# Inner norms of a two-layer decoder trunk: order of the first scaled and modulated pieces, a constant product on another engine, and eight instead of four weight units held back at the end

## The chip, the core and the metric

The kernel runs on one core of a Trainium2 chip. A core has five engines that run their own instruction lists in order and wait for each other by semaphores: TensorE (PE, matrix products and transposes; its weight loads are listed apart as PEld), VectorE (DVE), ScalarE (ACT), GpSimd (POOL) and SyncE (SP, which issues most transfers). Weights lie in HBM and come to the on-chip memory (SBUF) by DMA; TensorE writes its sums to eight banks of PSUM. The metric is the time of one execution in microseconds (us). The kernel before takes 2213.51 us (median of 3 runs, 2211.17 to 2214.28).

## What is computed

x has 256 rows (tokens) of 2048. Each of two layers has a token mixer (forgetting attention in layer 0, sliding-window attention in layer 1) and a gated feed-forward network with a causal convolution. Every such part is framed in the same way; the shift, scale and gate come from a conditioning vector c:

```python
c_act = jax.nn.silu(c)
for i in range(DEPTH):
    mod = c_act @ ada_w[i] + ada_b[i]
    sh1, sc1, g1, sh2, sc2, g2 = jnp.split(mod[:, None, :], 6, axis=-1)
    h = x * (1.0 + sc1) + sh1
    ...  # y = attention(h)
    x = layer_norm(DEEPNORM_ALPHA * x + (1.0 + g1) * y, ln_mix_g[i], ln_mix_b[i])
    h = x * (1.0 + sc2) + sh2
    y = conv_ffn(h, ffn_w_up[i], ffn_conv_w[i], ffn_conv_b[i], ffn_w_down[i])
    x = layer_norm(DEEPNORM_ALPHA * x + (1.0 + g2) * y, ln_ffn_g[i], ln_ffn_b[i])
return x
```

So there are four layer norms. After three of them, the inner ones, the normalised x is scaled, shifted and multiplied with the next weights; the last one gives the output.

## The kernel before

**Numbers in two parts.** All large products are made in a reduced float32 format. To keep the precision, each operand is split into a high part (the value cast to that format) and a low part (value minus high part), and a product is three matmuls: high by high, low by high, high by low. For a weight tile `w`, ScalarE makes the high part `wh` (a cast, line 268), VectorE the low part `wl` (a subtraction, line 279). In the activations the two halves are called hH and hL; both lie in one tile, `hpad`, and the profile names both "hH".

**Units.** Weights stream in units of 256 contraction rows by 512 columns (512 KB each). A unit is 24 matmuls of 256 columns where weights are stationary (`w_mm`, outputs named `ws`) or 12 matmuls of 512 columns where activations are (`x_mm`, outputs `xs`; six of them for each half t of the 256 tokens). Four buffers hold `wh` and four `wl`, so the cast of a unit waits until TensorE is done with the unit four places before. Ten buffers hold the raw weights.

**Order of the work.** The program is written by functions that queue work; a scheduler then fixes the order on each engine by its own estimates, except that instructions wrapped in `pin(...)` keep their program order among the pinned ones of their engine.

**An inner norm** runs at the three places where one part ends and the next begins. The last block's sum for token half t = 0 and then for t = 1 goes through `residual`: VectorE multiplies by the gate (line 632), adds to x (634), takes statistics (639, 642, 644), and GpSimd raises the variance to the power -1/2 (645). For t = 0 the product -mean times that factor (638) is made on VectorE, pinned between the two halves' work. `between` then calls `modulate`: x is normalised in four column blocks d of 512 (t = 0 on ScalarE, line 655; t = 1 on VectorE, line 657), TensorE transposes it in pieces of 128 by 128 (496; tile `sm`; a piece of 128 columns over both token halves is called a chunk here, there are 16), and `mod_pair` scales and shifts a chunk. For chunks 0 to 3 ScalarE writes hH straight from the transpose (506) and VectorE computes the value again (507) and subtracts (508) to get hL. For the later chunks, two at a time, ScalarE (510) and VectorE (511) make one chunk each, ScalarE casts both (84) and VectorE subtracts (85). These later pairs ("feeds") are queued one behind each unit of the next product. `spin` issues small matmuls without use on TensorE: three while it waits for the statistics, two behind the first transposes.

**The end.** In the last product of a part the last units are held back (`x_mm_end`): their matmuls for t = 0 run first, then those for t = 1, so that the residual of t = 0 runs beside the matmuls of t = 1. In the last product of the kernel four units are held. After the last residual the output is x minus mean, times gain (line 1180), times the factor, plus bias (1181), in four blocks for each t, each stored by a DMA.

Of the kernel before, what the change touches and what calls it, by code (L numbers as in the profile page):

```python
# [11 lines left out]
F32R = mybir.dt.float32r  # L12
I32 = mybir.dt.int32
AF = mybir.ActivationFunctionType
ALU = mybir.AluOpType
AX = mybir.AxisListType

P = 128
D = 2048
S = 256  # L20
# [21 lines left out]
def hybrid_trunk(ctx: ExitStack, tc: tile.TileContext, a: dict, out: bass.AP):  # L42
# [34 lines left out]
    def pin(ins, on=True):  # L77

        if on:
            tc.keep_in_program_order(ins)  # L80
# [176 lines left out]
        while post:  # L257
            run_post()

    def stream(wsrc, row0, col, ks, use):  # L260

        for kc in ks[::2]:
            r0 = (row0 + kc) * P
            w = wtile()
            pin(nc.sync.dma_start(w, wsrc[r0:r0 + 2 * P, col:col + WB].rearrange("(k p) f -> p k f", p=P)), False)
            h = hl.tile([P, 2, WB], F32R, tag="wh", name="wh")
            l = hl.tile([P, 2, WB], F32R, tag="wl", name="wl")
            pin(nc.scalar.copy(h, w), False)  # L268

            def go(kc=kc, h=h, l=l):  # L270
                ahead[0] -= 1
                run_post()
                use(kc, h, l)
                if feeds:
                    feeds.pop(0)()
                tick()

            def residual_(w=w, h=h, l=l, go=go):
                pin(nc.vector.tensor_tensor(l, w, f32(h), op=ALU.subtract), behind[0] > 0)  # L279
                behind[0] -= 1  # L280
                del residuals[go]

            ahead[0] += 1
            weights.add(go)
            residuals[go] = residual_
            work.append(go)
            settle(2)
# [25 lines left out]
    def w_mm(ps, kc, h, l, last=KC - 1, first=0):  # L313

        for i in range(2):
            for f in range(4):
# [3 lines left out]
                mm(o, wh, hL[:, kc + i, :], skip_group_check=True)  # L320
                mm(o, wl, hH[:, kc + i, :], stop=kc + i == last, skip_group_check=True)

    def x_stationary(wsrc, col, k0, nk, stat, end=0):

        ps = x_banks()
        use = x_mm_end(ps, stat, nk, end) if end else lambda kc, h, l: x_mm(ps, kc, h, l, stat, nk - 1)
        stream(wsrc, k0, col, list(range(nk)), use)
        return ps

    def w_stationary(wsrc, col):  # L330
# [166 lines left out]
            os.append(o)  # L497
        return os

    def mod_pair(G, B, k, ps, fast=False, keep=False):  # L500
        tmp = ttile()
        if fast:
            for j in range(2):
                o = tmp[:, j * S:(j + 1) * S]
                g, b = G[:, k + j:k + j + 1], B[:, k + j:k + j + 1]
                pin(nc.scalar.activation(hH[:, k + j, :], ps[j], AF.Identity, bias=b, scale=g), keep)
                nc.vector.tensor_scalar(o, ps[j], g, b, op0=ALU.mult, op1=ALU.add)
                nc.vector.tensor_tensor(hL[:, k + j, :], o, f32(hH[:, k + j, :]), op=ALU.subtract)
            return
        pin(nc.scalar.activation(tmp[:, :S], ps[0], AF.Identity, bias=B[:, k:k + 1], scale=G[:, k:k + 1]), keep)  # L510
        nc.vector.tensor_scalar(tmp[:, S:], ps[1], G[:, k + 1:k + 2], B[:, k + 1:k + 2],
                                op0=ALU.mult, op1=ALU.add)
        split(hH[:, k:k + 2, :], hL[:, k:k + 2, :], tmp.rearrange("p (j s) -> p j s", j=2))
# [4 lines left out]
    def spin(o, n):  # L518

        for _ in range(n):  # L520
            pin(mm(o[:, :3 * P], ident, mask.rearrange("p a b -> p (a b)"), start=True, stop=True))

    def modulate(G, B, norm, o=None):

        def feed(k):
            if k % 4 == 0:
                norm(k // 4)
            mod_pair(G, B, k, mod_turn(k, 2), k < 4)

        feeds.extend([lambda k=k: feed(k) for k in range(0, KC, 2)])  # L530
        for _ in range(2):
            feeds.pop(0)()
        spin(o, 2)

    def opening(plan, proj, prep):

# [92 lines left out]
    def residual(ps, d, gate, last):  # L629
        for t in range(NT):  # L630
            tmp = ttile()
            nc.vector.tensor_tensor(tmp, ps[t], gate[:, d * 512:(d + 1) * 512], op=ALU.mult)  # L632
            xs = x[:, t, d * 512:(d + 1) * 512]
            nc.vector.tensor_tensor(xs, xs, tmp, op=ALU.add)  # L634
            if last:
                if t == 1 and d == D // 512 - 1:
                    mu, rs, nm = moments[0]
                    pin(nc.vector.scalar_tensor_tensor(nm, mu, -1.0, rs, op0=ALU.mult, op1=ALU.mult))  # L638
                nc.vector.bn_stats(stats[:, t, d, :], xs)  # L639
                if d == D // 512 - 1:  # L640
                    mv = sp.tile([P, 2], F32, tag="mv", name="mv")
                    nc.vector.bn_aggr(mv, stats[:, t].rearrange("p a b -> p (a b)"))  # L642
                    rs = sp.tile([P, 2], F32, tag="rs", name="rs")
                    nc.vector.tensor_scalar_add(mv[:, 1:2], mv[:, 1:2], EPS)  # L644
                    nc.gpsimd.tensor_tensor(rs[:, 0:1], mv[:, 1:2], mhalf, op=ALU.pow)
                    moments[t] = (mv[:, 0:1], rs[:, 0:1], rs[:, 1:2])
            yield

    def normalise(d):

        for t in range(NT):
            mu, rs, nm = moments[t]
            xs = x[:, t, d * 512:(d + 1) * 512]
            if t == 0:
                nc.scalar.activation(xs, xs, AF.Identity, scale=rs, bias=nm)
            else:
                nc.vector.tensor_scalar(xs, xs, mu, rs, op0=ALU.subtract, op1=ALU.mult)

    def ln_rows(name, l):
        gb, bb = [], []  # L660
# [425 lines left out]
    def conv_ffn(l):  # L1086
        w_up, w_dn = a["ffn_w_up"][l], a["ffn_w_down"][l]
        NB = DFF // WB
        cw = lambda j, f: ccol[:, l, j, f:f + 1]

        def conv(pf, f):
            u = tp.tile([P, S], F32, tag="u", bufs=3, name="u")
            nc.scalar.activation(u, pf, AF.Identity, bias=cw(CW, f), scale=cw(2, f))  # L1093
            nc.vector.scalar_tensor_tensor(u[:, 1:], pf[:, :S - 1], cw(1, f), u[:, 1:],  # L1094
                                           op0=ALU.mult, op1=ALU.add)
            nc.vector.scalar_tensor_tensor(u[:, 2:], pf[:, :S - 2], cw(0, f), u[:, 2:],  # L1096
                                           op0=ALU.mult, op1=ALU.add)
            return u

        def evac(ps, f0, then):  # L1100
            u = None
            for f in range(5):
                v = conv(ps[f // 2][:, f % 2, :], f0 + f) if f < 4 else None
                if u is not None:
                    then(f - 1, u)
                u = v
                yield
                yield

        def silu(sil):  # L1110
            def f_(f, u):
                nc.scalar.activation(sil[f // 2][:, (f % 2) * S:(f % 2 + 1) * S], u, AF.Silu)
            return f_

        def gated(sil, gT):
            def f_(f, u):
                nc.vector.tensor_tensor(u, u, sil[f // 2][:, (f % 2) * S:(f % 2 + 1) * S], op=ALU.mult)
                g = gtile("gT")
                split(g[:, 0, :], g[:, 1, :], u)
                gT.append(g)  # L1120
            return f_

        sbs = [(0, 6), (6, NB)]
        for si, (b0, b1) in enumerate(sbs):
            gT = []
            then(lambda: ada.update(rate=(0.64, 0.4)[l]))
            for b in range(b0, b1):
                ps = w_stationary(w_up, b * WB)
                sil = [ttile("sil") for _ in range(2)]
                then(lambda ps=ps, b=b, sil=sil: defer(evac(ps, b * 4, silu(sil))))  # L1130
                ps = w_stationary(w_up, DFF + b * WB)
                then(lambda ps=ps, b=b, sil=sil, gT=gT: defer(evac(ps, DFF // P + b * 4, gated(sil, gT))))

            def stat(kc, t, gT=gT):
                while kc >= len(gT):
                    run_post()
                return gT[kc][:, 0, t * P:(t + 1) * P], gT[kc][:, 1, t * P:(t + 1) * P]

            def ready(si=si):
                if si == 0:  # L1140
                    drain()
                ada_need(l, 5)
                ada["rate"] = (0.95, 0.4)[l]

            then(ready)
            for d in range(D // WB):
                ps = x_stationary(w_dn, d * WB, b0 * 4, (b1 - b0) * 4, stat, (2, 4)[l] if si > 0 and d == D // WB - 1 else 0)
                then(lambda ps=ps, d=d, si=si: defer(residual(ps, d, gates[l, 5], si == len(sbs) - 1)),
                     si > 0 and d == D // WB - 1)
        then(lambda: (flush(), ada.update(gate_free=True)), True)  # L1150
# [58 lines left out]
```

## Time and profile before

| | |
|---|---|
| median of the runs shown | 2213.51 us |
| the profiled execution | 2215.89 us |
| its span, first to last instruction | 2214.0 us |
| TensorE busy | 2164.3 us (98%) |
| VectorE busy | 1792.8 us (81%) |
| ScalarE busy | 1159.6 us (52%) |
| GpSimd busy | 19.0 us (1%) |
| mean granted TensorE clock | 0.992 |

The three inner norms lie near 471, 1208 and 1470 us, the end near 2190 to 2214 us. A row of the timeline has the start, the length, the engine, the line, the operation, the tiles (written <- read), their shape and how many instructions are merged in it; in brackets stands how long the engine had been idle and what released it. The length of a merged row runs from the first start to the last end. Line numbers are those of the kernel before.

### The profile page before, as it was taken

How to read it: one execution, taken by the hardware profiler on the slowest of the kernel's cores; microseconds unless marked ns; L12 is line 12 of the kernel's file. 1: busy time of each engine (PE TensorE's matmuls, PEld its weight loads, DVE VectorE, ACT ScalarE, POOL GpSimd, SP SyncE). 2: the span in 40 equal slices, each digit the busy share in tenths (PEclk: the TensorE clock that was granted, in tenths of full speed). 3: DMA queues.
4: the chain of work that ended last, by engine and by line, in shares of the span. 5: the costliest groups of instructions: out<-in, count | busy, mean ns of one | idle time of the engine just before them, and what ended most of it. 6: DMA issues, size and time to landing. Idle time of an engine off the chain costs nothing. (4 is left out here: it accounts for less than half of the span.)

```text
span 2214.0 us, 38357 instructions
## 1 busy us (share of the span) xinstructions
PE 2164.3 (98%) x14915; PEld 1976.7 (89%) x14915; DVE 1792.8 (81%) x2459; ACT 1159.6 (52%) x1841; POOL 19.0 (1%) x48
## 2 busy tenths in 40 slices
PE   6999999999999999999999999999999999999997
PEld 5999888789999988999987877789999988999986
DVE  6879998989978979799798888789888655666756
ACT  3435656465565543655644677555555533555532
POOL 0000000000000000000000000000000000000000
PEclk9999999999999999999999999999999999999999
DMA  9999998979978989899797676678888566666663
GB/s 334 368 352 366 351 352 298 327 257 323 349 234 300 322 312 385 260 311 322 251 354 290 201 240 206 208 257 295 281 264 270 187 194 195 192 195 195 191 195 108
DMA packets 274246, 602.98 MB, mean 272 GB/s; under 512 B 21062, under 2 KB 29960, under 8 KB 273552
## 3 DMA queue, kind: packets, MB, share of 16 engines
q1 hardware_dynamic: 273008, 595.85, 79.6%
q0 software_dynamic: 1056, 4.69, 0.6%
q8 instruction: 116, 1.90, 0.3%
q14 instruction: 66, 0.54, 0.1%
HBM read 598.37 MB, written 2.10 MB: 271 GB/s over the span
## 5 line engine op out<-in xcount | busy, mean ns | idle before, releaser
L268 ACT CAST wh<-w 128x1024 fp32r<-128x1024 f32 x728 | 765.3, 1053 | 790.0 <-PE ws L75 284.5
L75 PE MATMUL ws<-hH,wh 128*128 128x256 f32 x6656 | 1153.3, 278 | 4.6 <-ACT hH L84 2.1
L279 DVE TENSOR_TENSOR wl<-w,wh 128x1024 fp32r<-128x1024 f32 x728 | 887.6, 1222 | 325.3 <-ACT wh L268 308.5
L75 PEld LDWEIGHTS ws<-hH,wh 128*128 128x128 f32 x6656 | 1012.1, 189 | 9.0 <-ACT hH L84 2.3
L75 PE MATMUL ws<-hH,wl 128*128 128x256 f32 x3328 | 918.6, 277 | 4.3 <-DVE wl L279 4.0
L75 PEld LDWEIGHTS ws<-hH,wl 128*128 128x128 f32 x3328 | 628.5, 189 | 6.0 <-DVE wl L279 5.9
L75 PE MATMUL xs<-wh,gT 128*128 128x512 f32 x1408 | 435.3, 389 | 0.0
L75 PEld LDWEIGHTS xs<-wh,gT 128*128 128x128 f32 x1408 | 264.3, 188 | 54.7
L75 PE MATMUL xs<-wl,gT 128*128 128x512 f32 x704 | 273.9, 389 | 0.0
L75 PE MATMUL xs<-wh,hH 128*128 128x512 f32 x704 | 235.9, 401 | 0.0
L397 DVE SCALAR_TENSOR_TENSOR acc<-wa,cact,acc 128x1024 f32<-128x1024 f32 x180 | 228.4, 1278 | 0.0
L397 DVE SCALAR_TENSOR_TENSOR acc<-wa,cactp,acc 128x1024 f32<-128x1024 f32 x128 | 162.3, 1278 | 0.3 <-DMA acc<-in_ada_b_dram 0.3
L75 PEld LDWEIGHTS xs<-wh,hH 128*128 128x128 f32 x704 | 131.3, 188 | 29.4 <-issue 0.7
L75 PEld LDWEIGHTS xs<-wl,gT 128*128 128x128 f32 x704 | 132.2, 188 | 27.4
L75 PE MATMUL xs<-wl,hH 128*128 128x512 f32 x352 | 138.7, 395 | 2.5 <-DVE wl L279 2.5
L1093 ACT ACTIVATE u<-ws,ccol 128x256 f32<-128x256 f32 x176 | 96.7, 562 | 58.5 <-PE ws L75 43.3
L75 PE MATMUL xs<-wh,oT 128*128 128x512 f32 x384 | 126.2, 397 | 0.8 <-ACT oT L84 0.8
L1094 DVE SCALAR_TENSOR_TENSOR u<-ws,ccol,u 128x255 f32<-128x255 f32 x176 | 82.6, 477 | 14.9 <-ACT u L1093 14.7
L75 PEld LDWEIGHTS xs<-wh,oT 128*128 128x128 f32 x384 | 72.1, 188 | 16.6 <-ACT oT L84 1.2
L1096 DVE SCALAR_TENSOR_TENSOR u<-ws,ccol,u 128x254 f32<-128x254 f32 x176 | 83.1, 477 | 2.2
L75 PEld LDWEIGHTS xs<-wl,hH 128*128 128x128 f32 x352 | 66.5, 189 | 17.5 <-DVE wl L279 4.3
L576 DVE SCALAR_TENSOR_TENSOR oacc<-wo,cact,oacc 128x1024 f32<-128x1024 f32 (+1 forms) x68 | 73.3, 1078 | 8.3 <-DMA wo<-in_ada_w_dram 7.1
(220 smaller groups left out, 1280.4 us busy)
## 6 DMA issues: line engine op xcount, KB each, us to landing
w<-in_ffn_w_up_dram SPq DMA_DIRECT2D x352, 512.0 KB, 4.7
wa<-in_ada_w_dram SPq DMA_DIRECT2D x320, 512.0 KB, 5.6
w<-in_ffn_w_down_dram SPq DMA_DIRECT2D x176, 512.0 KB, 4.9
w<-in_fox_w_in_dram SPq DMA_DIRECT2D x96, 512.0 KB, 6.9
wo<-in_ada_w_dram SPq DMA_DIRECT2D x48, 512.0 KB, 9.0
w<-in_swa_w_in_dram SPq DMA_DIRECT2D x40, 512.0 KB, 4.6
w<-in_fox_w_o_dram SPq DMA_DIRECT2D x32, 512.0 KB, 6.2
w<-in_swa_w_o_dram SPq DMA_DIRECT2D x32, 512.0 KB, 4.8
```

Of the source, the lines that this page charges most:

```text
L75: return nc.tensor.matmul(o, lhsT, rhs, start=start, stop=stop, **kw)
L268: pin(nc.scalar.copy(h, w), False)
L279: pin(nc.vector.tensor_tensor(l, w, f32(h), op=ALU.subtract), behind[0] > 0)
L397: pin(nc.vector.scalar_tensor_tensor(ac, wo, (cactp if row else cact)[:, k:k + 1], ac, op0=ALU.mult, op1=ALU.add), True)
L576: nc.vector.scalar_tensor_tensor(acc, w[:, k], cact[:, kc:kc + 1], acc, op0=ALU.mult, op1=ALU.add)
L1093: nc.scalar.activation(u, pf, AF.Identity, bias=cw(CW, f), scale=cw(2, f))
L1094: nc.vector.scalar_tensor_tensor(u[:, 1:], pf[:, :S - 1], cw(1, f), u[:, 1:], op0=ALU.mult, op1=ALU.add)
L1096: nc.vector.scalar_tensor_tensor(u[:, 2:], pf[:, :S - 2], cw(0, f), u[:, 2:], op0=ALU.mult, op1=ALU.add)
```

## The change

Six edits:

- `mod_pair` and `normalise` pin VectorE's and ScalarE's instructions that they issue for the norm (the first four chunks' lines 507 and 508, and lines 655 and 657). The four blocks d of the scaling are thereby issued where the program has them: block 0 first, the others with their feeds.
- For t = 1 block 0 is scaled in two instructions of 256 columns.
- The two `spin` products behind the first transposes stand one behind each of the first two feeds.
- The product of -mean and the factor for t = 0 is made on GpSimd directly behind the power, and is no longer on VectorE. This holds for all four norms.
- In layer 1's last product eight units are held back in place of four.
- For that, the `wh` and `wl` of the first four held units lie in the tile `hpad`, whose activations are not needed any more (`spares`).

```diff
@@ -257,14 +257,13 @@
-    def stream(wsrc, row0, col, ks, use):
+    def stream(wsrc, row0, col, ks, use, spare={}):
...
-            h = hl.tile([P, 2, WB], F32R, tag="wh", name="wh")
-            l = hl.tile([P, 2, WB], F32R, tag="wl", name="wl")
+            h, l = spare.get(kc) or (hl.tile([P, 2, WB], F32R, tag=n, name=n) for n in ("wh", "wl"))
             pin(nc.scalar.copy(h, w), False)
...
+    def spares(nk):
+        t = [hpad[:, 56 + i * 2 * WB:56 + (i + 1) * 2 * WB].rearrange("p (a f) -> p a f", a=2) for i in range(8)]
+        return {nk - 16 + 2 * i: (t[2 * i], t[2 * i + 1]) for i in range(4)}
...
-        stream(wsrc, k0, col, list(range(nk)), use)
+        stream(wsrc, k0, col, list(range(nk)), use, spares(nk) if end == 8 else {})
...
-                nc.vector.tensor_scalar(o, ps[j], g, b, op0=ALU.mult, op1=ALU.add)
-                nc.vector.tensor_tensor(hL[:, k + j, :], o, f32(hH[:, k + j, :]), op=ALU.subtract)
+                pin(nc.vector.tensor_scalar(o, ps[j], g, b, op0=ALU.mult, op1=ALU.add), fixed)
+                pin(nc.vector.tensor_tensor(hL[:, k + j, :], o, f32(hH[:, k + j, :]), op=ALU.subtract), fixed)
...
-            mod_pair(G, B, k, mod_turn(k, 2), k < 4)
+            mod_pair(G, B, k, mod_turn(k, 2), k < 4, False, k < 4)
...
         for _ in range(2):
             feeds.pop(0)()
-        spin(o, 2)
+            spin(o, 1)
...
-                if t == 1 and d == D // 512 - 1:
-                    mu, rs, nm = moments[0]
-                    pin(nc.vector.scalar_tensor_tensor(nm, mu, -1.0, rs, op0=ALU.mult, op1=ALU.mult))
...
                     nc.gpsimd.tensor_tensor(rs[:, 0:1], mv[:, 1:2], mhalf, op=ALU.pow)
+                    if t == 0:
+                        nc.gpsimd.tensor_scalar(rs[:, 1:2], mv[:, 0:1], rs[:, 0:1], -1.0, op0=ALU.mult, op1=ALU.mult)
...
-                nc.scalar.activation(xs, xs, AF.Identity, scale=rs, bias=nm)
+                pin(nc.scalar.activation(xs, xs, AF.Identity, scale=rs, bias=nm))
             else:
-                nc.vector.tensor_scalar(xs, xs, mu, rs, op0=ALU.subtract, op1=ALU.mult)
+                for xp in ([xs[:, :S], xs[:, S:]] if d == 0 else [xs]):
+                    pin(nc.vector.tensor_scalar(xp, xp, mu, rs, op0=ALU.subtract, op1=ALU.mult))
...
-                ps = x_stationary(w_dn, d * WB, b0 * 4, (b1 - b0) * 4, stat, (2, 4)[l] if si > 0 and d == D // WB - 1 else 0)
+                ps = x_stationary(w_dn, d * WB, b0 * 4, (b1 - b0) * 4, stat, (2, 8)[l] if si > 0 and d == D // WB - 1 else 0)
```

What the scheduler makes of it differs at two kinds of places. In these lists the lines of the changed kernel stand up to three higher than before (496 is 499, 510 is 513, 655 is 657, 268 is 267; the output's 1180 and 1181 are 1183 and 1184).

TensorE at the first inner norm, before: the spins, then the first matmuls of unit 0 (`wh_4889`) and the transposes for chunks 4 to 6 (`sm_5013` is chunk 4, `sm_5014` chunk 5, `sm_5056` chunk 6, two token halves each).

```order
L75 MATMUL spin_4946<-mask_86,ident_81 128x384 x2
L75 MATMUL ws_4885<-hH_129,wh_4889 128x256
L75 MATMUL ws_4886<-hH_129,wh_4889 128x256
L496 MATMUL sm_5013<-ident_81,x_108 128x128 x2
L496 MATMUL sm_5014<-ident_81,x_108 128x128 x2
L496 MATMUL sm_5056<-ident_81,x_108 128x128 x2
```

After, chunk 4 is `sm_5014` and chunk 5 `sm_5015`; the first halves of their transposes stand behind all 24 matmuls of unit 0, and these are the second halves, inside unit 1 (`wh_4901`, `wl_4902`) with its last six matmuls behind them.

```order
L75 MATMUL ws_4885<-hH_129,wl_4902 128x256
L499 MATMUL sm_5014<-ident_81,x_108 128x128
L499 MATMUL sm_5015<-ident_81,x_108 128x128
L75 MATMUL ws_4886<-hH_129,wh_4901 128x256 x2
L75 MATMUL ws_4886<-hH_129,wl_4902 128x256
```

The transposes of chunks 4 and 5 thus moved from behind two matmuls of unit 0 to behind its end and 18 matmuls of unit 1.

ScalarE at the same place, before, from the last block of the scaling on: `t_5019` holds chunks 4 and 5, `wh_5069` is the cast of the unit that takes unit 0's buffer, `wh_5112` the one that takes unit 1's.

```order
L655 ACTIVATE x_108<-x_108,rs_4933 128x512
L510 ACTIVATE t_5019<-sm_5013,B_4951,G_4950 128x256
L510 ACTIVATE t_5062<-sm_5056,B_4951,G_4950 128x256
L268 CAST wh_5069<-w_5067 128x1024
L84 CAST hH_129<-t_5019 128x512
L268 CAST wh_5112<-w_5110 128x1024
```

After, `t_5020` holds chunks 4 and 5, and `wh_5070` and `wh_5113` are these two casts.

```order
L267 CAST wh_5070<-w_5068 128x1024
L657 ACTIVATE x_108<-x_108,rs_4933 128x512
L513 ACTIVATE t_5020<-sm_5014,B_4951,G_4950 128x256
L267 CAST wh_5113<-w_5111 128x1024
L84 CAST hH_129<-t_5020 128x512
```

The cast that needs unit 1's buffer moved ahead of the one that writes hH of chunks 4 and 5.

VectorE at the end of the kernel, before: the residual of t = 1 (632, 634, 639) among the output of t = 0.

```order
L632 TENSOR_TENSOR t_23876<-xs_23654,gate_19182 128x512
L1181 SCALAR_TENSOR_TENSOR x_108<-x_108,rs_23873,ln_23892 128x512
L634 TENSOR_TENSOR x_108<-x_108,t_23876 128x512
L638 SCALAR_TENSOR_TENSOR rs_23873<-mv_23871,rs_23873 128x1
L1180 SCALAR_TENSOR_TENSOR x_108<-x_108,mv_23871,ln_23890 128x512
L639 BN_STATS stats_130<-x_108 128x6
```

After:

```order
L1183 SCALAR_TENSOR_TENSOR x_108<-x_108,mv_23866,ln_23885 128x512 x2
L1184 SCALAR_TENSOR_TENSOR x_108<-x_108,rs_23868,ln_23887 128x512 x2
L635 TENSOR_TENSOR t_23872<-xs_23657,gate_19185 128x512
L637 TENSOR_TENSOR x_108<-x_108,t_23872 128x512
L639 BN_STATS stats_130<-x_108 128x6
```

The whole output of t = 0 moved ahead of the residual of t = 1.

2 lines of the change are left out of this document (1 added, 1 removed).

## The prediction

> **What bounds the kernel now.** I read the page first, then the timeline at the three inner norms and at the end, the only places where the order differs.
>
> ```profile
> span 2214.0 us, 38357 instructions
> ```
>
> TensorE is busy for 98% of this span, so what counts is where TensorE waits, and the tail behind its last matmul. The execution took 2215.89 us, 1.9 around its span and 2.4 above the median of 2213.51; changes are summed against it and laid on the median.
>
> At the first norm (timeline; POOL is GpSimd):
>
> ```profile
> 471.26 0.57 POOL L645 TENSOR_TENSOR rs<-mv,mhalf 128x1 f32<-128x1 f32 x1 [15.38 <-DVE mv L644]
> 472.67 0.15 DVE L638 SCALAR_TENSOR_TENSOR rs<-mv,rs 128x1 f32<-128x1 f32 x1
> ...
> 474.05 0.55 POOL L645 TENSOR_TENSOR rs<-mv,mhalf 128x1 f32<-128x1 f32 x1 [2.22 <-DVE mv L644]
> 474.64 1.92 DVE L657 TENSOR_SCALAR x<-x,mv,rs 128x512 f32<-128x512 f32 x4 [0.67 <-POOL rs L645]
> 475.24 0.66 PE L496 MATMUL sm<-ident,x 128*128 128x128 f32 x4 [0.85 <-DVE x L657]
> 475.61 1.93 ACT L506 ACTIVATE hH<-sm,B,G 128x256 fp32r<-128x256 f32 x4 [0.52 <-PE sm L496]
> 475.74 1.46 PE L75 MATMUL spin<-mask,ident 128*128 128x384 f32 x4
> 476.47 0.99 DVE L507 TENSOR_SCALAR t<-sm,G,B 128x256 f32<-128x256 f32 x2
> 476.73 0.70 PE L75 MATMUL ws<-hH,wh 128*128 128x256 f32 x2
> 477.27 0.82 PE L496 MATMUL sm<-ident,x 128*128 128x128 f32 x6
> 477.38 0.75 DVE L508 TENSOR_TENSOR hH<-t,hH 128x256 fp32r<-128x256 f32 x2
> 478.07 0.28 PE L75 MATMUL ws<-hH,wl 128*128 128x256 f32 x1
> ```
>
> VectorE's chain for t = 1 sets the start: power, scaling, transposes. Two spins keep TensorE until about 477.04 (four pieces of 0.325 from 475.74). hL of chunk 0 comes near 477.8, but six transposes fill that gap.
>
> ```profile
> 479.62 2.35 DVE L279 TENSOR_TENSOR wl<-w,wh 128x1024 fp32r<-128x1024 f32 x2
> 480.38 0.28 PE L75 MATMUL ws<-hH,wl 128*128 128x256 f32 x1
> 482.52 0.62 ACT L84 CAST hH<-t 128x512 fp32r<-128x512 f32 x1 [0.84 <-DVE t L511]
> 483.04 0.39 PE L75 MATMUL ws<-hH,wh 128*128 128x256 f32 x2
> 483.46 1.05 ACT L268 CAST wh<-w 128x1024 fp32r<-128x1024 f32 x1 [0.32 <-PE ws L75]
> 483.48 0.69 DVE L85 TENSOR_TENSOR hH<-t,hH 128x512 fp32r<-128x512 f32 x1
> 484.22 0.38 PE L75 MATMUL ws<-hH,wh 128*128 128x256 f32 x1
> 484.42 0.56 ACT L510 ACTIVATE t<-sm,B,G 128x256 f32<-128x256 f32 x1
> 492.68 0.60 PE L496 MATMUL sm<-ident,x 128*128 128x128 f32 x4
> ```
>
> The fourth matmul of unit 0 starts at 478.07, its 24th at 480.38: 0.1155 each, 2.77 a unit; six transposes take (0.82 - 0.27) / 5 = 0.11 each. Unit 2 needs chunks 4 and 5: hH is there at 483.14 (482.52 + 0.62), hL at 484.17 (483.48 + 0.69), and its third matmul starts at 484.22. So unit 2 is fed just in time. Unit 4 ends at 492.68, with 16 of the 24 later transposes done.
>
> **The first norm, walked through.**
>
> 1. Line 638 leaves VectorE's chain: 0.12 (0.15 less overlap). The power starts at 473.93, the scaling at 474.52. The half block (256 columns, not in the trace) lies between the 0.15 of line 638 and a whole block (1.92 / 4 = 0.48); by its size I take 0.3. TensorE's transposes for t = 1 start at 474.89 instead of 475.24.
> 2. Two transposes, a spin, two transposes, a spin: 0.22 + 0.65 + 0.22 + 0.65, so unit 0 starts at 476.63, not 477.04. hL of chunk 0 needs 0.37 (475.61 - 475.24) and about 0.95 (a pair of 0.99 / 2 and 0.75 / 2, each with some 0.05 of latency) more, and is there by 476.3. This gains 0.4.
> 3. But only the first block is scaled; the six transposes now come later. Unit 0 ends at 479.40. Four transposes and 18 matmuls follow (0.44 + 2.08): the second halves for chunks 4 and 5 start at 481.92, some 4 us later than before (477.3 to 478.1). Six matmuls and six more transposes then last until 483.49.
> 4. ScalarE has the cast for unit 1's buffer ahead of hH. Before, that cast came 0.31 after the start of the last matmul with `wh` (the second of 483.04, at 483.15), and the next instruction 0.96 later. Now: 482.60 + 0.31 = 482.91, hH from 483.87 to 484.49. TensorE, free at 483.49, waits until 484.56, 1.1 us, for two matmuls.
> 5. VectorE: four pairs 507/508 of 0.91 (two took 1.66, 476.47 to 478.13, with scalings and subtractions overlapping; now each subtraction waits for its own scaling) from 475.26 to 478.9, two subtractions of 1.13 (2.35 for two that overlap), a block 0.48, a third subtraction 1.13, two times 0.48 for line 511, a fourth 1.13: 484.85. Then hL, 0.69, and 0.06 to TensorE (475.24 less 474.64 and a block): 485.6, another 0.8 us of waiting behind the two matmuls.
> 6. Unit 2's other 22 matmuls end at 488.13, unit 3 at 488.13 + 0.22 + 2.77 = 491.12. For unit 4 the same chain (last `wh` matmul of unit 2 at 487.90, + 0.31 + 0.96 + 0.46 for line 510 + 0.72 for the moved last block of 655, each its row less overlap, + 0.62 + 0.03 + 0.69 + 0.06) gives hL at 491.75, 0.3 after TensorE is there. It ends at 494.41 with the same 16 transposes done: **1.7 us later** than 492.68. Behind it both orders are alike, and TensorE has no slack to give it back.
>
> The product on GpSimd is bounded by the shortest and the longest similar row:
>
> ```profile
> L127 POOL TENSOR_SCALAR cactp<-cact x1: 276/276/276, 4.1 to 4.1; 128x16 f32<-128x16 f32 x1
> ```
>
> 0.28 to 0.98 (the power at 2197.55, below). t = 0's block 0 needs 0.80 + 0.07 + 0.44 after it and is due at 474.89; the power ends at 471.83, so up to 1.7 is hidden. The cast that now stands between it and line 506 ends by 474.8 even then; 475.26 is its due time. I take 0. The two powers differ by 0.4 us: 0.55 beside idle VectorE, 0.93 beside line 1180, which reads two SBUF tiles. The Trainium skill (SBUF — State Buffer, "SBUF: two separate sides") says that GpSimd and such a VectorE instruction exclude each other on a shared port, whoever starts first; both rows agree. By it the new product, started near 471.9, would hold line 634 (472.06) by 0.1 to 0.4 at two norms, and the sum below would be 0.2 to 0.8 higher.
>
> **The second and third norm.**
>
> ```profile
> 1212.59 1.46 PE L75 MATMUL spin<-mask,ident 128*128 128x384 f32 x4
> 1226.32 0.60 PE L496 MATMUL sm<-ident,x 128*128 128x128 f32 x4
> 1229.52 0.60 PE L496 MATMUL sm<-ident,x 128*128 128x128 f32 x4
> ...
> 1470.78 0.26 ACT L443 ACTIVATE sm<-sm 128x128 f32<-128x128 f32 x1
> 1471.18 0.26 ACT L443 ACTIVATE sm<-sm 128x128 f32<-128x128 f32 x1
> 1471.45 0.80 ACT L655 ACTIVATE x<-x,rs 128x512 f32<-128x512 f32 x1
> 1474.74 1.46 PE L75 MATMUL spin<-mask,ident 128*128 128x384 f32 x4
> 1492.00 0.60 PE L496 MATMUL sm<-ident,x 128*128 128x128 f32 x4
> ```
>
> Second (xs, 12 matmuls of 0.23 a unit: 1229.52 - 1226.32 = 3.20 less four transposes): it starts 0.4 earlier, at 1213.50. Four matmuls of unit 2 need no hL, so it waits 1.2 for hH and hardly for hL; for unit 4 0.1 more. It ends at 1230.33 against 1229.52: **+0.8**. Third: four line-443 sums of 0.40 now precede block 0, which ends at 1473.18, and unit 0 starts at 1475.43 instead of 1476.04 (1474.74 + 1.30). The steps of the first norm, 998.80 later, end unit 4 at 1493.21 against 1492.00: **+1.2**. Together **+3.7**.
>
> **The end.**
>
> ```profile
> 2194.78 0.69 DVE L632 TENSOR_TENSOR t<-xs,gate 128x512 f32<-128x512 f32 x1 [3.13 <-PE xs L75]
> 2197.25 0.15 DVE L644 TENSOR_SCALAR mv<-mv 128x1 f32<-128x1 f32 x1
> 2197.55 0.93 POOL L645 TENSOR_TENSOR rs<-mv,mhalf 128x1 f32<-128x1 f32 x1 [724.44 <-DVE mv L644]
> 2199.79 0.39 PE L75 MATMUL xs<-wh,gT 128*128 128x512 f32 x1
> 2200.63 0.68 DVE L632 TENSOR_TENSOR t<-xs,gate 128x512 f32<-128x512 f32 x1
> 2204.77 0.15 DVE L644 TENSOR_SCALAR mv<-mv 128x1 f32<-128x1 f32 x1
> ```
>
> TensorE's last result is there at 2200.22, but VectorE begins t = 1's residual at 2200.63, behind t = 0's output, and needs 4.14 to line 644 with three of t = 0's instructions and line 638 in between; t = 0's residual alone took 2.47. With eight units held, t = 0 is ready 8 x 1.36 = 10.9 before TensorE's end and needs 2.5 + 8 x 0.66, so VectorE is idle by then. Gain: 0.41 + 1.67 = **2.1**. The first four held units must come early: their casts stand up to two places ahead, and the transfer of the last depends on a buffer freed some 5 us before,
>
> ```profile
> w<-in_ffn_w_down_dram SPq DMA_DIRECT2D x176, 512.0 KB, 4.9
> ```
>
> so the unit behind it is cast up to 3 us later. ScalarE works 1.05 of 2.76 a unit and stands over 5 us ahead of TensorE: nothing.
>
> Sum: 3.7 - 2.1 = +1.6; 2213.51 becomes **2215.1 us**, or 2217.5 for the profiled execution.
>
> **Rivals.**
>
> *The waits for unit 2 do not come* (the schedule's slack is greater than I count): then 0.4 + 0.4 + 0.6 + 2.1 are gained: 2210.0. For it: the start is surely earlier. Against it: steps 4 and 5 are fixed orders, and hL would have to come 1.9 us earlier.
>
> *TensorE's clock halves after the new waits*, which ends slower.
>
> ```profile
> 163.16:166.57 3.41, 3.41 (x18) 3.41 (x18) 3.41 (x5) 1.32 (x2) 0.00 (x0) 0.50 0.92 270
> 473.77:477.19 3.42, 2.57 (x14) 1.80 (x15) 2.72 (x8) 2.90 (x6) 0.55 (x1) 1.00 0.01 2
> ```
>
> (PE, PEld, DVE, ACT, POOL busy, clock.) A stretch of 3.41 us at half clock has occurred; 0.85 idle in such a stretch at the norm did not bring one. The new waits put up to 1.4 idle into one. A drop costs 3.41 / 2 = 1.7; one at the first and one at the third norm give 2215.1 + 3.4 = 2218.5. It decides from two drops on. The Trainium skill (TensorE: Matmul & The Clock Gate, "Part 1") wants an idle window of about 3.4 us for that; by it no drop, 2215.1.
>
> *The held units starve TensorE* (the early casts delay the others by more than 5 us): no gain at the end and some loss, 2217 to 2219. Against it: the ten buffers.
>
> **How the numbers follow.** 0.2% (4.4 us, about what a measurement of this kernel can tell from no change) sets the bounds at 2209.1 and 2217.9. Chances: forecast 0.62, no waits 0.14, clock 0.14, starved 0.10. The forecast's own range is 2212.5 to 2217.5 (the port, the half block, 0.5 for each norm); with no waits below and the clock above it, 2209.5 to 2218.9. Runs differ by 3 us, so each case has a tail: faster takes 0.06 of the no-waits case and 0.05 of the forecast; slower 0.10 of the clock's case, 0.06 of the starved one and 0.08 of the forecast; the rest, 0.65, is within.
>
> **What would show it.** Right: TensorE waits of about 1 us for line 84 and of up to 1 us for line 85, some 7 us after each norm's first matmul; the first matmul 0.4 to 0.6 earlier after the transposes; the tail from the last matmul's end 2 us shorter, line 632 without output lines behind it. Wrong: no such waits, half clock near 485 or 1484 us, or gaps in TensorE between 2177 and 2200.

## The result

| | before | changed |
|---|---|---|
| median | 2213.28 us (9 runs) | 2218.78 us (9 runs) |
| lowest to highest | 2211.17 to 2215.98 | 2214.95 to 2221.37 |
| the profiled execution | 2215.89 | 2220.91 |
| its span | 2214.0 | 2218.5 |

The changed kernel is slower: ratio 1.0023, interval 1.0014 to 1.0031, some 5 us. The forecast was 2215.1 us, 1.6 over before, and a range of 2209.5 to 2218.9. The medians of the kernel before were 2213.27 to 2213.99 in the sessions of the experiments, so each kernel below is set against the one of its own session.

**Where the time is.** The page of the changed kernel begins

```profile
span 2218.5 us, 38352 instructions
...
PE 2167.3 (98%) x14915; PEld 1976.6 (89%) x14915; DVE 1795.2 (81%) x2458; ACT 1159.4 (52%) x1841; POOL 21.4 (1%) x52
```

and shows no new bound. To place 4.5 us, cut both spans at the same events: the first `spin` of each inner norm, which stands directly behind the last matmul of the product before, and the start of the last matmul of all. From the timelines (TensorE's rows; start, length), before:

```profile
471.14 2.10 PE L75 MATMUL spin<-mask,ident 128*128 128x384 f32 x6
...
1208.01 2.10 PE L75 MATMUL spin<-mask,ident 128*128 128x384 f32 x6
...
1470.06 2.10 PE L75 MATMUL spin<-mask,ident 128*128 128x384 f32 x6
```

and after:

```profile
471.26 2.10 PE L75 MATMUL spin<-mask,ident 128*128 128x384 f32 x6
...
1210.85 2.10 PE L75 MATMUL spin<-mask,ident 128*128 128x384 f32 x6
...
1474.65 2.10 PE L75 MATMUL spin<-mask,ident 128*128 128x384 f32 x6
...
2206.33 0.39 PE L75 MATMUL xs<-wh,gT 128*128 128x512 f32 x1
```

Each of the three stretches between these begins with a norm and goes on with products whose work the change leaves alone (the last one only runs its last units in another order). The last matmul of before starts at 2199.79. So:

| | before | changed | difference |
|---|---|---|---|
| up to the first norm | 471.14 | 471.26 | +0.12 |
| first norm to second | 736.87 | 739.59 | +2.72 |
| second to third | 262.05 | 263.80 | +1.75 |
| third to the last matmul | 729.73 | 731.68 | +1.95 |
| tail, from the start of the last matmul | 14.21 | 12.17 | -2.04 |
| span | 2214.0 | 2218.5 | +4.5 |

The end gained its 2 us. The norms lost 6.4 where 3.7 was forecast. (The medians differ by 1.0 more than the spans do; the last section says where executions differ.)

**The first norm after the change** (chosen rows of the timeline; from the start it runs 0.12 later than before):

```profile
472.19 0.69 DVE L637 TENSOR_TENSOR x<-x,t 128x512 f32<-128x512 f32 x1
472.91 0.69 DVE L639 BATCH_NORM_STATS2 stats<-x 128x6 f32<-128x512 f32 x1
474.76 0.73 DVE L660 TENSOR_SCALAR x<-x,mv,rs 128x256 f32<-128x256 f32 x2 [0.67 <-POOL rs L645]
475.23 0.44 PE L499 MATMUL sm<-ident,x 128*128 128x128 f32 x2 [1.35 <-DVE x L660]
475.60 1.93 ACT L509 ACTIVATE hH<-sm,B,G 128x256 fp32r<-128x256 f32 x4 [1.50 <-PE sm L499]
476.19 0.55 DVE L510 TENSOR_SCALAR t<-sm,G,B 128x256 f32<-128x256 f32 x1 [0.70 <-ACT hH L509]
476.77 0.42 DVE L511 TENSOR_TENSOR hH<-t,hH 128x256 fp32r<-128x256 f32 x1
477.12 0.54 DVE L510 TENSOR_SCALAR t<-sm,G,B 128x256 f32<-128x256 f32 x1
479.52 0.43 DVE L511 TENSOR_TENSOR hH<-t,hH 128x256 fp32r<-128x256 f32 x1
479.86 2.35 DVE L278 TENSOR_TENSOR wl<-w,wh 128x1024 fp32r<-128x1024 f32 x2
480.04 0.38 PE L499 MATMUL sm<-ident,x 128*128 128x128 f32 x2
481.14 0.39 PE L75 MATMUL ws<-hH,wl 128*128 128x256 f32 x1
482.87 0.38 PE L499 MATMUL sm<-ident,x 128*128 128x128 f32 x2
483.93 1.04 ACT L267 CAST wh<-w 128x1024 fp32r<-128x1024 f32 x1 [0.18 <-PE ws L75]
484.88 0.62 ACT L84 CAST hH<-t 128x512 fp32r<-128x512 f32 x1
485.55 0.50 PE L75 MATMUL ws<-hH,wh 128*128 128x256 f32 x2 [0.90 <-ACT hH L84]
486.56 0.39 PE L75 MATMUL ws<-hH,wh 128*128 128x256 f32 x1 [0.51 <-DVE hH L85]
495.54 0.60 PE L499 MATMUL sm<-ident,x 128*128 128x128 f32 x4
```

The forecast's waits are there: TensorE stands 0.90 us for hH of chunks 4 and 5 (line 84, behind the cast of 483.93, which needs the buffer of unit 1) and, two matmuls later, 0.51 for hL. But all of it is later than forecast, and the reason stands higher up. VectorE's first residual (line 510) starts at 476.19, not when the transposes are there (475.6) but 0.02 after ScalarE's first hH (475.60 + 0.57); the four pairs of lines 510 and 511 run without a gap to 479.95. The list of waits of this norm has, in the rows of TensorE's weight loads (us in total, times, longest), two smaller ones from the same cause, for hL of chunk 0 and for unit 1's `wl`:

```profile
PEld ws L75 <- ACT hH L84: 1.1, 1, 1.1
PEld ws L75 <- DVE hH L85: 1.0, 2, 0.7
...
PEld ws L75 <- DVE hH L511: 0.4, 1, 0.4
PEld ws L75 <- DVE wl L278: 0.3, 1, 0.3
```

**The end after the change**: line 635 starts right behind the last matmul, and nothing of t = 0's output is among t = 1's residual any more, which takes 2.47 us to line 644:

```profile
2206.76 0.69 DVE L635 TENSOR_TENSOR t<-xs,gate 128x512 f32<-128x512 f32 x1 [2.95 <-PE xs L75]
2207.48 0.69 DVE L637 TENSOR_TENSOR x<-x,t 128x512 f32<-128x512 f32 x1
...
2209.23 0.15 DVE L644 TENSOR_SCALAR mv<-mv 128x1 f32<-128x1 f32 x1
```

### The profile page after: what moved, and what is told of

Same layout as the page of the kernel before. It is cut to its first block, busy times and chain, and to the rows that moved or that the text cites. A ratio compares the mean times of both kernels' runs of the same rounds, so it can differ in the third digit from the quotient of the medians.

```text
span 2218.5 us, 38352 instructions
## 1 busy us (share of the span) xinstructions
PE 2167.3 (98%) x14915; PEld 1976.6 (89%) x14915; DVE 1795.2 (81%) x2458; ACT 1159.4 (52%) x1841; POOL 21.4 (1%) x52
## 4 chain that ended last, share of the span: by engine, by line
PE 70%; DVE 6%; ACT 2%; issue 1%; DMA 0%; DVEq 0%; POOL 0%; ACTq 0%
PE ws L75 41%; PE xs L75 27%; DVE wl L278 2%; DVE acc L400 1%; ACT wh L267 1%; ACT pr L1062 0%; PE sm L442 0%; DMA wa<-in_ada_w_dram 0%; DVE pr L708 0%; DVE t L510 0%; ACT pr L712 0%; PE sm L75 0%; DVE hH L511 0%; PE sm L499 0%; DMA w<-in_ffn_w_up_dram 0%
## 5 line engine op out<-in xcount | busy, mean ns | idle before, releaser
L75 PE MATMUL xs<-wh,gT 128*128 128x512 f32 x1376 | 425.7, 389 | 0.0
L75 PEld LDWEIGHTS xs<-wh,gT 128*128 128x128 f32 x1376 | 258.3, 188 | 53.5
L75 PE MATMUL xs<-wl,gT 128*128 128x512 f32 x688 | 267.7, 389 | 0.0
```

The costliest lines, as they stand in the source:

```text
L75: return nc.tensor.matmul(o, lhsT, rhs, start=start, stop=stop, **kw)
```

## The experiments

For every kernel the same four cuts are read from its timeline. They repeat within 0.15 us wherever the code is the same (before, and with the end alone changed: first stretch 736.87 and 736.89, second 262.05 and 261.90, third 729.73 twice; tails with four held units 14.16 to 14.24), so they tell apart what whole executions, which scatter by 3 us and more, do not. "Norms" is the sum of the three stretches less that of before (1728.65).

| | first | second | third | norms | tail | ratio to before |
|---|---|---|---|---|---|---|
| before | 736.87 | 262.05 | 729.73 | 0 | 14.21 | |
| changed | 739.59 | 263.80 | 731.68 | +6.42 | 12.17 | 1.0023 (1.0014 to 1.0031) |
| 1 end alone | 736.89 | 261.90 | 729.73 | -0.13 | 12.12 | 0.9989 (0.9980 to 0.9998) |
| 2 norms alone | 739.62 | 263.84 | 731.68 | +6.49 | 14.16 | 1.0028 (1.0016 to 1.0040) |
| 3 all but the pins | 736.79 | 262.37 | 730.81 | +1.32 | 12.12 | 1.0000 (0.9991 to 1.0009) |
| 4 pins alone | 739.73 | 264.00 | 731.90 | +6.98 | 14.23 | 1.0035 (1.0023 to 1.0048) |
| 5 pins on the scaling | 739.18 | 263.70 | 731.32 | +5.55 | 14.24 | one execution |
| 6 pins on the residuals | 736.98 | 261.90 | 729.71 | -0.06 | 14.23 | one execution |
| 7 changed, first residual free | 739.12 | 263.42 | 731.16 | +5.05 | 12.12 | one execution |
| 8 half block, spins, end | 736.79 | 261.89 | 729.46 | -0.51 | 12.16 | 0.9986 (0.9977 to 0.9995) |
| 9 changed, block 1 early | 737.61 | 262.35 | 729.41 | +0.72 | 12.16 | 0.9997 (0.9988 to 1.0006) |
| 10 changed, all blocks first | 736.23 | 262.62 | 729.61 | -0.19 | 12.21 | 0.9987 (0.9978 to 0.9996) |
| 11 as 10, product on VectorE | 736.21 | 262.08 | 729.61 | -0.75 | 12.15 | 0.9987 (0.9978 to 0.9996) |

The theory at this point: the pins, because block 1 of the scaling then comes behind the first residuals, carry the loss. The rivals: the other edits of the norms share it, the serial residuals carry it, or the loss beyond the forecast belongs to that one execution.

**1 and 2: the two halves of the change.** The first is the kernel before with this alone (and with `stream` and `spares` as in the change):

```diff
-                ps = x_stationary(..., (2, 4)[l] if si > 0 and d == D // WB - 1 else 0)
+                ps = x_stationary(..., (2, 8)[l] if si > 0 and d == D // WB - 1 else 0)
...
-        stream(wsrc, k0, col, list(range(nk)), use)
+        stream(wsrc, k0, col, list(range(nk)), use, spares(nk) if end == 8 else {})
```

> The kernel before with the end alone changed: eight units held, their first four wh and wl in hpad. Theory 'tail': the changed kernel's trace has 12.17 us from the start of the last matmul to the end of the span against 14.21 before, and the same 704.6 us from the last transposes to the last matmul, so this kernel is 2.0 us faster than before, 0.1% (ratio 0.9991), and its norms are those of before. Rival 'held units starve TensorE': the end gains nothing, 0 to +2 us, with gaps in TensorE after 2175 us.

Median 2211.55 against 2213.89. The norms are those of before and the tail is 2.09 shorter; no stretch is longer by more than 0.02, so no unit starves. The second is the changed kernel with four held units:

```diff
-                ps = x_stationary(..., (2, 8)[l] if si > 0 and d == D // WB - 1 else 0)
+                ps = x_stationary(..., (2, 4)[l] if si > 0 and d == D // WB - 1 else 0)
```

> All edits of the three norms (pins, half block, one spin behind each feed, product on GpSimd), four units held as before. Theory 'norms': TensorE loses 2.7, 1.8 and 1.9 us at the three norms, so +6.5 us over before (ratio 1.0029); the last matmul starts 6.5 us later and the tail is that of before, 14.2 us. Rival 'the 2.8 us missing from my forecast are a state of the run': +3.7 us, as predicted, ratio 1.0017.

Median 2220.27. The loss is there again to 0.1 us, stretch by stretch. It belongs to the program, and the two halves add up: 6.49 - 2.09 = 4.40, measured together 6.42 - 2.04 = 4.38.

**3 and 4: with and without the pins.** Number 3 is the changed kernel without its pins (`pin(...)` taken off lines 510, 511, 657 and 660); number 4 is the kernel before with them alone:

```diff
-                nc.scalar.activation(xs, xs, AF.Identity, scale=rs, bias=nm)
+                pin(nc.scalar.activation(xs, xs, AF.Identity, scale=rs, bias=nm))
...
-                nc.vector.tensor_scalar(xs, xs, mu, rs, op0=ALU.subtract, op1=ALU.mult)
+                pin(nc.vector.tensor_scalar(xs, xs, mu, rs, op0=ALU.subtract, op1=ALU.mult))
...
-                nc.vector.tensor_scalar(o, ps[j], g, b, op0=ALU.mult, op1=ALU.add)
-                nc.vector.tensor_tensor(hL[:, k + j, :], o, f32(hH[:, k + j, :]), op=ALU.subtract)
+                pin(nc.vector.tensor_scalar(o, ps[j], g, b, op0=ALU.mult, op1=ALU.add), fixed)
+                pin(nc.vector.tensor_tensor(hL[:, k + j, :], o, f32(hH[:, k + j, :]), op=ALU.subtract), fixed)
```

> The changed kernel without its pins on the scalings of x and on the first four chunks' residuals: half block, split spins, GpSimd product and eight held units stay. The transposes of chunks 4 and 5 then stand behind two matmuls of unit 0, as before. Theory 'pins': the loss at the norms is gone, and with the end's 2.0 and up to 0.4 from each start this is 2 to 3 us faster than before (ratio 0.9987 to 0.9991). Rival 'other norm edits': the split spins, the half block or the product keep at least half of the loss, +1 us or more against before (ratio over 1.0004).

> The kernel before with nothing but the pins: scaling of x (both halves) and the first four chunks' residuals in program order; four whole blocks, spins together, product on VectorE, four units held. Theory 'pins': they carry the whole loss, +6 to +7 us (ratio 1.0027 to 1.0032), with TensorE's waits of about 0.9 us for line 84 behind each norm. Rival 'other norm edits': under +3.5 us.

The pins alone lose 6.98, a little more than all the edits of the norms together, and TensorE waits 0.9, 1.0 and 0.9 us for line 84 behind the three norms. Without them the first norm is that of before. But number 3 came out neither way: median 2215.21 against 2213.89, ratio 1.0000, since the second stretch keeps 0.32 and the third 1.08. The third norm in its timeline (chosen rows):

```profile
1472.54 1.03 ACT L267 CAST wh<-w 128x1024 fp32r<-128x1024 f32 x1
1473.47 0.26 ACT L446 ACTIVATE sm<-sm 128x128 f32<-128x128 f32 x1
...
1474.46 0.26 ACT L446 ACTIVATE sm<-sm 128x128 f32<-128x128 f32 x1
1476.05 0.17 DVE L696 TENSOR_TENSOR B<-B,cv 128x16 f32<-128x16 f32 x1
1476.31 1.93 ACT L509 ACTIVATE hH<-sm,B,G 128x256 fp32r<-128x256 f32 x4 [0.77 <-DVE B L696]
1476.93 0.51 PE L75 MATMUL ws<-hH,wh 128*128 128x256 f32 x2 [1.55 <-ACT hH L509]
```

ScalarE sums four columns here (line 446, 443 before) that the shift B and the gain G need. With the product on GpSimd the scheduler has put a weight cast ahead of the last two sums, so B, the first hH and TensorE's unit 0 are late: a wait of 1.55 us that before does not have. In the changed kernel the pins hold all four sums together ahead of the scaling, and this does not happen.

**5 and 6: which pins.** Number 5 has only the first two lines of the diff above (the scaling), number 6 only the last two (the residuals).

> The kernel before with only the scalings of x pinned (both halves), not the first chunks' residuals. Measure: time from the first spin of a norm to the four transposes behind unit 5; before it is 24.74, 24.72 and 25.18 us, with all pins 27.61, 26.73, 27.31. Theory 'late transposes': here too those of chunks 4 and 5 stand behind unit 0 and inside unit 1, so nearly the whole loss comes back: 27.0 to 27.6, 26.3 to 26.7, 26.8 to 27.3. Rival 'serial residuals' (VectorE's pairs one after another make hL late): at most a third of the loss, 25.7, 25.4, 25.9 or less.

> The kernel before with only the first four chunks' residuals pinned, not the scalings. The transposes of chunk 4 stay behind two matmuls of unit 0. Same measure. Theory 'late transposes': at most a third of the loss, 25.7, 25.4, 25.9 or less. Rival 'serial residuals': 26.5, 26.0, 26.5 or more.

The scaling pins lose 5.55 alone (the first of the two theories: in the measure of the expectation 27.06, 26.35 and 26.74 us, the last 0.06 below the range given); the residual pins nothing, 24.86, 24.70 and 25.01 us in that measure. Together they lose 1.5 more than their sum: VectorE's serial pairs cost something only where the transposes of chunks 4 and 5 are late already.

**7: the wait of the first residual.** The changed kernel with

```diff
+                src = x[:, 1, :S] if fixed and k + j == 0 else ps[j]
-                pin(nc.vector.tensor_scalar(o, ps[j], g, b, op0=ALU.mult, op1=ALU.add), fixed)
+                pin(nc.vector.tensor_scalar(o, src, g, b, op0=ALU.mult, op1=ALU.add), fixed)
```

> The changed kernel with one instruction of each norm altered: the first of the lines that compute the residual's value (chunk 0) reads 256 columns of x in place of the transposes, so that it needs not wait for ScalarE's hH of the same chunk; the low half of chunk 0 is therefore wrong. Some transposes shift by a few matmuls with it. Same measure; the changed kernel has 27.48, 26.56, 27.11. Theory 'VectorE's late start' (the 0.6 us that this line waits for ScalarE is what my forecast missed, and runs through the pairs to wl and hL): 0.4 to 0.6 shorter at each norm. Rival 'the cast decides' (hH of chunks 4 and 5 waits for TensorE's end of unit 1 and ScalarE's cast): under 0.2 shorter.

This kernel leaves out the true low half of chunk 0 (it subtracts from another value). Line numbers are one higher in the timeline (511 is 510, 512 is 511, 661 is 660):

```profile
469.59 0.73 DVE L661 TENSOR_SCALAR x<-x,mv,rs 128x256 f32<-128x256 f32 x2 [0.68 <-POOL rs L646]
470.24 0.41 DVE L511 TENSOR_SCALAR t<-x,G,B 128x256 f32<-128x256 f32 x1
470.43 1.93 ACT L509 ACTIVATE hH<-sm,B,G 128x256 fp32r<-128x256 f32 x4 [1.50 <-PE sm L499]
471.02 0.42 DVE L512 TENSOR_TENSOR hH<-t,hH 128x256 fp32r<-128x256 f32 x1 [0.38 <-ACT hH L509]
```

The first residual now runs beside ScalarE's, the subtraction follows 1.43 after the scaling's start (2.01 in the changed kernel, 474.76 to 476.77), and the stretches are 0.47, 0.38 and 0.52 shorter: 1.37 in all. (In the measure of the expectation it is 0.49, 0.37 and 0.53.) That is what the first theory said at two norms and just under it at the second; the rival said under 0.2. Part of it may come from the transposes that moved with it; the two were not taken apart.

**8: the early start without the pins.** The kernel before with the half block, one spin behind each feed, and the end; no pins, and the product on VectorE.

> The kernel before with the half block, one spin behind each feed and the end's eight held units; no pins, product on VectorE. Theory: the earlier start of unit 0 is taken back at unit 2, which is fed just in time, so the norms are within 0.2 us of before, and the end gives 2.0: ratio 0.9988 to 0.9992. Rival 'the start counts': 0.3 to 0.5 less at each norm, 3 us faster in all, ratio 0.9985 or less. If the third norm is over 0.5 longer, as it is with the product on GpSimd (26.28 against 25.18), then the product has no part in that.

The first stretch hardly changes (-0.08), although the first pair of t = 1's transposes comes 0.14 earlier (3.96 us behind the first spin against 4.10); the second and third gain 0.16 and 0.27, the second no more than number 1 differs from before there. The theory holds at two norms; at the third it is 0.07 more than its 0.2, and the ratio, 0.9986, lies between the theory's range and the rival's. Median 2210.90 against 2213.27. Against number 3, which differs only in the product, the second stretch is 0.48 and the third 1.35 shorter: without the pins it is the product on GpSimd that costs.

**9, 10 and 11: pins kept, blocks moved.** Number 9 is the changed kernel with block 1 scaled directly behind block 0, number 10 with all four blocks there:

```diff
-            if k % 4 == 0:
-                norm(k // 4)
+            for d in {0: (0, 1), 8: (2,), 12: (3,)}.get(k, ()):      # number 9
+            for d in range(4 if k == 0 else 0):                      # number 10
+                norm(d)
```

> The changed kernel, pins and all, with one call moved: the scaling of column block 1 stands directly behind that of block 0, ahead of the first chunks' residuals; blocks 2 and 3 stay with their feeds. The transposes of chunks 4 and 5 can then stand directly behind unit 0, and hH of chunks 4 and 5 needs no cast that waits for unit 1. Measure: from the first spin of a norm to that of the next, and from the third norm's to the last matmul; before 736.87, 262.05 and 729.73 us, changed 739.59, 263.80 and 731.68. Theory 'block 1 comes too late': under 40% of the loss stays, 737.9, 262.7, 730.5 or less, and with the end's 2.0 the kernel is 0 to 2 us faster than before (ratio 0.999 to 1.0). Rival 'pairs, spins or product': over 60% stays, 738.5, 263.1, 730.9 or more, ratio over 1.0008.

> The changed kernel, pins and all, with all four column blocks scaled ahead of the first residuals, as the scheduler has them in the kernel before. Same measure. Theory 'block 1 comes too late': each stretch within 0.8 us of before (the serial pairs and the product still cost something), ratio 0.9988 to 1.0. Rival 'the pins themselves cost, wherever the blocks stand': 738.0, 262.9, 730.7 or more.

Moving one block takes 5.7 of the 6.42 away, with every pin, spin and product where the change has them. In number 9's list of waits for the first norm TensorE no longer waits for lines 84 and 85; behind the start, what is left is the wait for hL of chunk 0:

```profile
PEld ws L75 <- DVE hH L511: 0.4, 1, 0.4
```

Number 10 is in all three stretches within 0.8 of before, the first even 0.64 shorter; its ratio, 0.9987, is 0.0001 under the range given. Number 11 is number 10 with the product on VectorE:

```diff
-                    if t == 0:
-                        nc.gpsimd.tensor_scalar(rs[:, 1:2], mv[:, 0:1], rs[:, 0:1], -1.0, op0=ALU.mult, op1=ALU.mult)
...
+                if t == 1 and d == D // 512 - 1:
+                    mu, rs, nm = moments[0]
+                    pin(nc.vector.scalar_tensor_tensor(nm, mu, -1.0, rs, op0=ALU.mult, op1=ALU.mult))
```

> As the kernel with all four blocks scaled first (pins, half block, split spins, eight held units), but the product of -mean and factor stays on VectorE as before. In the same measure (spin to spin, third spin to last matmul) that kernel had 736.23, 262.62 and 729.61 us, and half block, split spins and end without pins 736.79, 261.89 and 729.46. Theory 'the product on GpSimd costs at the second norm' (0.81 us there beside line 637, and the scheduler sets a cast ahead of line 509): the second stretch falls to 261.9 to 262.2, the others stay within 0.2; ratio 0.9984 to 0.9990. Rival 'serial pairs cost there': the second stretch stays at 262.5 or more, ratio 0.9987 to 0.9995.

The second stretch falls by 0.54 to 262.08, the others stay. Numbers 1, 8, 10 and 11 are all faster than both kernels (8, 10 and 11 by medians of 2.4, 3.2 and 3.4 us against before; among them the intervals do not decide). By the cuts, number 11 has the shortest three stretches, 0.75 under before, and a tail shorter by 2.06.

## Why the prediction was right and wrong

The sign, the places and the two mechanisms (waits at unit 2, a shorter end) were right; the size was not: +1.6 forecast, about +5 measured. The range holds the 2218.78 by 0.12 us, and that is luck: its upper end was set by the rival of the halved clock, which did not occur (below), and the forecast's own range ended at 2217.5. The chances gave 0.65 to a change within 0.2% and 0.24 to a loss over it; the ratio, 1.0023, lies just above that bound, and its interval reaches to both sides of it.

- **The end** (-2.1 forecast): -2.04 in the changed kernel, -2.09 alone. Both parts came as worked out (residual right behind the last matmul; 2.47 us to line 644). The rival of starving units fell: the stretch to the last matmul is unchanged in number 1.
- **The waits for unit 2** (steps 3 to 5): right in place, order and cause. Forecast 1.1 and 0.8 us at the first norm, measured 0.90 and 0.51; for line 84 1.0 and 0.9 at the other two. Numbers 5, 9 and 10 show the cause: the place of block 1 of the scaling.
- **The early start** (steps 1 and 2: 0.4, 0.4 and 0.6 us): failed at the first two norms. Line 638 freed nothing: the statistics follow 0.72 behind the addition (472.19, 472.91), and followed 0.73 behind it with line 638 between them (rows of before, below). The half block gave 0.13 (scaling to transposes 0.47 against 0.60). What such a start is worth by itself number 8 hardly tells: its gains of 0.08, 0.16 and 0.27 are not far from the 0.15 within which the cuts repeat.

```profile
472.06 0.69 DVE L634 TENSOR_TENSOR x<-x,t 128x512 f32<-128x512 f32 x1
472.67 0.15 DVE L638 SCALAR_TENSOR_TENSOR rs<-mv,rs 128x1 f32<-128x1 f32 x1
472.79 0.69 DVE L639 BATCH_NORM_STATS2 stats<-x 128x6 f32<-128x512 f32 x1
```

- **VectorE's pairs from 475.26 on** (step 5), with hL of chunk 0 "by 476.3" (step 2): this step failed, and with it the size. They started at 476.19 - 0.12 = 476.07, 0.8 late, 0.6 of it because line 510 waits until ScalarE's line 509 has read the same transposes. The wait was in the kernel before as well, hidden behind the three further blocks of the scaling (its line 507 starts at 476.47, and the four blocks ran until 476.56): the pins took that cover away, and the forecast costed it at nothing. Number 7 puts it at up to 1.37 us over the three norms, half of the 2.7 that were missing. Of the other half (0.55, 0.57 and 0.23 by norm) some 0.27 at each of the first two is, as an estimate from the spins' rows, the start that did not come (the last spin ends 0.14 and 0.11 earlier, 0.4 was forecast); the rest was not taken apart.
- **From there on** each step is late by what it inherits. The cuts of the forecast, moved by the 0.12 of this execution: end of unit 0 at 479.52, measured 480.04; second halves of chunks 4 and 5 at 482.04, measured 482.87 (0.3 of it the wait for unit 1's `wl`, 481.14, which the forecast left out); hL at 485.72, measured 486.56; end of unit 4 at 494.53, measured 495.54.
- **The product on GpSimd** (forecast 0): with all blocks first it cost nothing at the first and third norm, where the stretches of numbers 10 and 11 agree within 0.02, and 0.54 at the second; in the changed kernel itself it was not tried alone. (Its upper bound, 0.98, is not the power at 2197.55, whose row has 0.93, but the longest one; the sum does not depend on it.) The Trainium skill's rule of the shared port (SBUF — State Buffer, "SBUF: two separate sides"), by which the product would hold line 634, is half borne out by these rows: the product took 0.26 us at the first norm, where it began 0.14 before line 637 (472.19), and 0.81 at the second, where it began 0.07 before it; line 637 came 0.73 behind line 635 there, as line 639 comes 0.72 behind line 637 at the first norm with GpSimd idle. So GpSimd's row grew and VectorE's spacing did not, though GpSimd began first by the rows; spans on GpSimd are rough.

```profile
472.05 0.26 POOL L647 TENSOR_SCALAR rs<-mv,rs 128x1 f32<-128x1 f32 x1
...
1211.05 0.69 DVE L635 TENSOR_TENSOR t<-xs,gate 128x512 f32<-128x512 f32 x1
1211.71 0.81 POOL L647 TENSOR_SCALAR rs<-mv,rs 128x1 f32<-128x1 f32 x1
1211.78 0.69 DVE L637 TENSOR_TENSOR x<-x,t 128x512 f32<-128x512 f32 x1
```

- **The rival of the halved clock** (2218.5 us) would have given the measured time, and is wrong. In the stretch of the two waits TensorE was idle for 1.41 of 3.42 us, and the granted clock there was 1.00, as it is on average in each of the three stretches (PE, PEld, DVE, ACT, POOL busy, clock):

```profile
484.01:487.43 3.42, 2.01 (x15) 1.57 (x14) 3.28 (x6) 2.57 (x4) 0.00 (x0) 1.00 0.87 267
```

A time that fits is not a mechanism that fits. The Trainium skill's longer idle window (TensorE: Matmul & The Clock Gate, "Part 1") agrees with this row.

## What to carry to other kernels

When an edit lets an engine go on earlier, ask what ran in the gap: here three column blocks of scaling stood ahead of the residuals, hid a wait of theirs, and fed the unit after next; putting them behind saved 0.1 us at the start and cost some 2 us ten microseconds later. Before costing a moved instruction from its operands alone, list every semaphore it waits on, those for engines that only read the same data too. And cut two traces at the same events: differences of 0.3 us per stage were plain there when whole executions scatter by 3 and more.

## What the runs showed of the hardware

**Two readers of one PSUM tile are kept apart.** In the changed kernel VectorE's read of the transposes (line 510, 476.19) starts 0.02 after ScalarE's read of the same tile ends, with nothing else to wait for; with another source (number 7) it runs beside it. The Trainium skill (PSUM — Partial Sum Buffer, "PSUM bank collisions raise a hardware error") says why a program has such a wait: two engines must not access one bank of PSUM in the same partitions at once, reads against reads included, so instructions on different engines that do are ordered. The trace agrees as to the order; what happens without it no run here shows.

**Executions differ ahead of the first norm, and hardly behind it.** The first spin came between 466.08 and 472.64 us in these profiled executions (the two below had the same number of instructions on every engine up to there), while the later stretches of the same code repeat within 0.15. The granted clock goes with it. Before, and number 7 (windows up to the first spin and from there to the last matmul; the sixth figure is the clock):

```profile
0.00:471.14 471.14, 442.12 (x2821) 399.45 (x2822) 407.72 (x529) 237.25 (x425) 12.63 (x38) 0.97 0.97 344
471.14:2199.80 1728.66, 1721.79 (x12095) 1577.28 (x12093) 1374.70 (x1913) 922.35 (x1416) 5.42 (x9) 1.00 0.76 254
```

```profile
0.00:466.08 466.08, 437.22 (x2821) 394.23 (x2822) 407.58 (x529) 237.68 (x425) 12.70 (x38) 0.99 0.98 348
466.08:2199.78 1733.70, 1723.97 (x12095) 1577.43 (x12093) 1379.12 (x1917) 923.42 (x1416) 7.77 (x13) 1.00 0.77 254
```

In slices of 3.41 us these first parts hold half-clock windows that add up to seven before and to four in number 7. The 5.06 us between the two are, as an estimate from the window of 3.41 us at half clock that the prediction shows, three such windows, 1.7 each. Over all kernels the count goes from four (466.08 and 467.13 us) to eight (471.60 and 472.64), but two with six lie 2.9 us apart (468.37 and 471.28), so the clock is not the whole of it. Such differences are enough to move the medians of one kernel by the 0.7 us seen between sessions, though no run shows that they do, and they are why number 7's single time, 2214.01, says nothing of its 5 us of loss.
